# The S5 gate projection as seven block products, with its weight sums made in DRAM

## The chip, the cores and the metric

One core of one Trainium2 chip runs the whole layer. The metric is the device time of one execution in microseconds (us); the kernel before took 1628.49 us, the median of three runs (1626.33 to 1628.78).

## The reference

The kernel computes one decoder layer for 1024 tokens of width 1024, in float32: an S5 branch and an mLSTM branch side by side, merged by gates, then `w_out`, cross-attention to 256 memory tokens and a convolutional FFN. The part that the change touches, cut from the reference:

```python
h = _rmsnorm(x, mix_norm_g[l])
proj = h @ w_in[l]
u_s5, q_in, k_in, v_in, o_in, i_pre, f_pre, gate_pre = jnp.split(proj, split_points, axis=-1)
y_s5 = _s5(u_s5, ...)      # ends in y * sigmoid(y @ w_glu + b_glu)
y_m = _mlstm(q_in, k_in, v_in, o_in, i_pre, f_pre, ...)
gates = jax.nn.sigmoid((gate_pre + b_gate[l]).astype(jnp.float32)).astype(x.dtype)
g_s5, g_m = jnp.split(gates, 2, axis=-1)
merged = g_s5 * (y_s5 @ w_br_s5[l]) + g_m * (y_m @ w_br_m[l])
x = x + merged @ w_out[l]
```

`gate_pre` has 2048 columns: 1024 for the S5 branch and 1024 for the mLSTM branch.

## The kernel before

Activations lie transposed: a tile has 128 features in its partitions and the 1024 tokens along its free dimension. A float32 product is made of three fp32r products, high by high, high by low and low by high. `split` makes the two parts of an operand: ACT casts it to the high part, DVE subtracts that from it for the low part. The input h is kept as eight such pairs, `hx`, of x times its norm gain; the factor of the norm, a row `rb` of one number per token, is multiplied onto the product later.

`ntile` makes one output tile of 128 columns: `load_w` fetches 512 KB of weights by a DMA on SP's queue into a buffer `WR` and splits it into `WH` and `WL` (two buffers of each), and PE runs 8 blocks x 3 products x 2 halves of 512 tokens = 48 matmuls into `M`, a PSUM tile of 1024 columns of which there are two. With `nk=4` (`w_br`, `w_glu`, whose inputs are 512 wide) there are 24 matmuls and 256 KB. PSUM tiles `A` of 512 columns, four of them, serve the small products. S, R, Z, Y and VV are pools of SBUF tiles.

`gate_tile(i, n)` is one tile of `gate_pre` (i is 0 for S5, 1 for mLSTM): `ntile`, times `rb`, plus bias, sigmoid. `merge_tile(i, n)` takes such a gate and multiplies it by the tile of `y @ w_br`; for i = 0 it adds the mLSTM part and splits the sum for `w_out`.

The table `ORDER` lists the steps of the first part of the kernel: p, r the S5 scan in four parts (`s5_params`, `s5_run`), v, g, j, m the mLSTM (`v_half`, `gate_rows`, `proj_head`, `mlstm_head`), s and y splits of the branch outputs (`ym_split`; `y_load` fetches the S5 output from `Yd` in DRAM and applies Gelu), and a0 to a7 the mLSTM merges with their gates. Behind the table follow S5 gate tile 0, the four glu tiles, S5 gate tile 1 and the eight S5 merges, each with its gate tile ahead of it from the third on. From this order and a cost model a scheduler sets the fixed sequence of instructions on each engine; an engine runs its own list strictly in order, and so does each engine's list of DMA issues.

In the FFN, products of 2x2 blocks are already made as seven products for eight (`Uq` and `Dd` hold sums of weight quarters). `quad_sums` makes such sums in DRAM without an engine's arithmetic: four DMA copies of a quarter (512 KB each) on POOL's queue, then four DMAs that accumulate another quarter or an earlier sum onto them, the last two after one another. The copies are held back until `last_mm`, the last weight matmul written before them, is done. Before the change two sets of Uq follow a5 and a7, and the four of Dd the second, fourth, sixth and eighth S5 merge.

A line number of the new file is up to 10 higher than the old one ahead of the gate code and more behind it (`ntile`'s matmuls are L214 before and L224 after, `quad_sums` L850 and L853 before and L965 after).

Of the kernel before, what the change touches and what calls it, by code (L numbers as in the profile page):

```python
# [88 lines left out]
def hybrid_layer(ctx: ExitStack, tc: tile.TileContext, a):  # L91
# [124 lines left out]
    def ntile(src, xs, nk=KD, width=T):  # L216

        wh, wl = load_w(src, (nk, P))
        ps = psM()
# [575 lines left out]
        return ymt  # L795

    def gate_tile(i, n):
        ps = ntile(a["w_in"][13 + 8 * i + n], hx)
# [1 line left out]
        V.tensor_tensor(out=gt, in0=ps, in1=rb, op=ALU.mult)  # L800
        A.activation(out=gt, in_=gt, func=AF.Sigmoid, bias=col("b_gate", 8 * i + n))
# [4 lines left out]

    def merge_tile(i, n, ys, gt=None):
        gt = gt or gate_tile(i, n)
        pb = ntile(a["w_br"][i, n], ys, nk=4)
        if i == 1:  # L810
            merged.append([Y(), Y()])
            for j in range(2):
                hs = slice(512 * j, 512 * j + 512)
                V.tensor_tensor(out=merged[n][j], in0=gt[:, hs], in1=pb[:, hs], op=ALU.mult)
            return
        hi, lo = S(F32R) if n < 4 else Z(F32R), Halves([Y(F32R), Y(F32R)])
        for j in range(2):
# [2 lines left out]
            V.tensor_tensor(out=gt[:, hs], in0=gt[:, hs], in1=pb[:, hs], op=ALU.mult)  # L820
# [26 lines left out]
    def quad_sums(dst, src, jj, starts, sums, after, w=slice(0, T)):

        for i, q in enumerate(starts):
            d = nc.gpsimd.dma_start(out=dst[jj, :, i, w], in_=src[jj, :, q, w])  # L850
            tc.add_manual_dep(d.ins, after.ins.name, DependencyInfo(DependencyClass.Sync, DependencyReason.DATA), reason="pace")
        for i, q in enumerate(sums):
            nc.gpsimd.dma_start(out=dst[jj, :, i, w], in_=src[jj, :, q, w] if i < 2 else dst[jj, :, q, w], accum_op=ALU.add)  # L853
# [7 lines left out]
    def up_sums(g):  # L861
        quad_sums(Uq, a["w_uq"], g, (1, 0, 0, 2), (3, 1, 0, 2), last_mm[0])

    for step in ORDER:
        i = int(step[1])
        if step[0] == "p":
            prm[i] = s5_params(i)
        elif step[0] == "r":
            s5_run(i, *prm[i])
        elif step[0] == "v":  # L870
            v_half(i)
        elif step[0] == "g":
            gate_rows()
        elif step[0] == "j":
            hp[i] = proj_head(i)
        elif step[0] == "m":
            ymf[i] = mlstm_head(i, *hp[i])
        elif step[0] == "s":
            ym_split(i)
        elif step[0] == "y":  # L880
            y_load(i)
        else:
            merge_tile(1, i, [ym[h] for h in range(NH)])
            if step in UP_SUMS_AT:
                up_sums(UP_SUMS_AT.index(step))


    ysp = [ysp[j] for j in range(4)]
    early = [gate_tile(0, 0)]
    y2 = []  # L890
    for j in range(4):
        ps = ntile(a["w_glu"][j], ysp, nk=4)
        hi, lo = (S(F32R), S(F32R)) if j < 2 else (VV(F32R)[:, :T], VV(F32R)[:, :T])
        for i in range(2):
            hs = slice(512 * i, 512 * i + 512)
            A.activation(out=ps[:, hs], in_=ps[:, hs], func=AF.Sigmoid, bias=col("b_glu", j))
            y_ = ysp[j][2][:, hs]
            V.tensor_tensor(out=y_, in0=y_, in1=ps[:, hs], op=ALU.mult)
            split(hi[:, hs], lo[:, hs], y_)
        y2.append((hi, lo))  # L900
    early.append(gate_tile(0, 1))
# [766 lines left out]
```

## Time and profile before

| what | value |
|---|---|
| median of 3 runs | 1628.49 us (1626.33 to 1628.78) |
| the profiled execution | 1622.69 us, span 1620.9 us, mean granted clock 0.996 |
| PE busy | 1597.7 us, 99% of the span |
| DVE, ACT, POOL busy | 1056.6, 700.7, 144.1 us |
| mLSTM with the projections in it | about 155.8 to 330 us of the span |
| mLSTM merges and the last S5 part | about 330 to 445.1 us |
| S5 gates, glu, S5 merges | 445.1 to 597.7 us |
| w_out and cross-attention begin | 597.7 us |

The page is of one execution. The row of an instruction group reads: line, engine, operation, output tile <- input tiles, shape, count, then busy us and mean ns of one, then the idle time of that engine just before them with what ended it. A row of the timeline gives the start in us, the duration in us, the instruction and, in brackets, the idle time ahead of it. PE is TensorE, PEld its weight loads, DVE VectorE, ACT ScalarE, POOL GpSimd, SP SyncE.

### The profile page before, as it was taken

The page shows a single profiled execution, that of the slowest core. Times are in us where ns is not written, and L with a number is a line of the kernel's source. Part 1 is how long each engine was busy: PE and PEld are TensorE (multiplying, and loading weights), DVE is VectorE, ACT ScalarE, POOL GpSimd, SP SyncE. Part 2 cuts the span into 40 slices and gives each one's busy share as a digit, 9 for nine tenths or more (in the row PEclk, how much of TensorE's full clock was granted, in tenths as well). Part 3 has the DMA queues.
Part 4 walks back from the last instruction along what each step waited for, and adds up shares of the span by engine and source line. Part 5 has one row for each costly group of instructions (what it writes and reads, how often), then busy time and mean ns, then how long its engine had stood idle before and what let it go on. Part 6 is the DMA issues. An engine that isn't in the chain of part 4 may idle for free.

```text
span 1620.9 us, 20862 instructions
## 1 busy us (share of the span) xinstructions
PE 1597.7 (99%) x8031; PEld 1347.7 (83%) x8031; DVE 1056.6 (65%) x1698; ACT 700.7 (43%) x1153; POOL 144.1 (9%) x216
## 2 busy tenths in 40 slices
PE   9999999999999999999999999999999999999997
PEld 7898888888888888888888888888887888888887
DVE  7878767675344434344466468788889878867535
ACT  6446545633432223343354346444434445543423
POOL 0000000000111112100000000000111011221014
PEclk9999999999999999999999999999999999999998
DMA  5231211313665688953205244532677375886312
GB/s 198 95 97 57 79 53 59 86 46 104 175 156 149 161 252 240 292 132 107 97 29 206 104 156 163 198 108 78 190 183 196 109 181 172 309 284 207 119 39 105
DMA packets 87653, 233.83 MB, mean 144 GB/s; under 512 B 9601, under 2 KB 23617, under 8 KB 87553
## 3 DMA queue, kind: packets, MB, share of 16 engines
q1 hardware_dynamic: 58528, 138.73, 25.7%
q0 software_dynamic: 21488, 75.25, 18.7%
q10 hardware_dynamic: 7536, 18.52, 3.1%
q8 instruction: 63, 1.03, 0.3%
q14 instruction: 38, 0.30, 0.1%
HBM read 201.53 MB, written 85.46 MB: 177 GB/s over the span
## 4 chain that ended last, share of the span: by engine, by line
PE 93%; DVE 2%; issue 1%; DMA 1%; ACT 1%; SPq 0%; POOL 0%; POOLq 0%; DVEq 0%; ACTq 0%
PE M L214 41%; PE A L1208 14%; PE M L1208 10%; PE M L1352 6%; PE A L1352 5%; PE A L214 4%; PE M L299 1%; PE A L1074 1%; PE A L1020 1%; PE A L994 1%; PE M L614 1%; PE M L616 1%; PE M L615 1%; PE A L299 1%; DMA S<-in_w_up_dram 1%
## 5 line engine op out<-in xcount | busy, mean ns | idle before, releaser
L214 PE MATMUL M<-S,WH 128*128 128x512 f32 (+1 forms) x1704 | 459.6, 382 | 1.9 <-DVE dc L787 1.4
L214 PEld LDWEIGHTS M<-S,WH 128*128 128x128 f32 x1704 | 312.9, 188 | 63.0 <-issue 2.1
L214 PE MATMUL M<-S,WL 128*128 128x512 f32 (+1 forms) x884 | 277.5, 381 | 0.0
L186 ACT CAST WH<-WR 128x1024 fp32r<-128x1024 f32 (+2 forms) x107 | 99.4, 930 | 326.6 <-PE M L214 246.9
L214 PEld LDWEIGHTS M<-S,WL 128*128 128x128 f32 x884 | 165.8, 188 | 31.5 <-DVE WL L187 0.5
L187 DVE TENSOR_TENSOR WL<-WR,WH 128x1024 fp32r<-128x1024 f32 (+2 forms) x107 | 114.7, 1072 | 74.9 <-ACT WH L186 73.6
L1208 PE MATMUL M<-S,Y 128*128 128x512 f32 x468 | 112.2, 389 | 0.8 <-DVE Z L1221 0.8
L1208 PEld LDWEIGHTS M<-S,Y 128*128 128x128 f32 x468 | 87.8, 188 | 19.3 <-DVE Z L1221 1.1
L1231 DVE SCALAR_TENSOR_TENSOR S<-Z,cols,S 128x1023 f32<-128x1023 f32 (+1 forms) x72 | 90.8, 1278 | 7.2 <-ACT S L1229 7.2
L1208 PE MATMUL M<-S,W 128*128 128x512 f32 x324 | 78.3, 389 | 0.0
L186 ACT CAST W<-Y 128x512 fp32r<-128x512 f32 x51 | 31.4, 620 | 97.4 <-PE A L1208 67.4
L800 DVE TENSOR_TENSOR R<-M,R 128x1024 f32<-128x1024 f32 x16 | 19.6, 1222 | 82.6 <-PE M L214 82.6
L1208 PEld LDWEIGHTS M<-S,W 128*128 128x128 f32 x324 | 60.8, 188 | 12.6
L1208 PE MATMUL A<-S,W 128*128 128x512 f32 x288 | 70.6, 389 | 0.0
L1208 PEld LDWEIGHTS A<-S,W 128*128 128x128 f32 x288 | 54.1, 188 | 11.2
L1208 PE MATMUL A<-S,Y 128*128 128x512 f32 x240 | 60.1, 389 | 0.0
L1352 PE MATMUL M<-S,W 128*128 128x512 f32 x240 | 57.8, 389 | 0.0
L1208 PE MATMUL A<-R,W 128*128 128x512 f32 x228 | 56.5, 391 | 0.6 <-ACT Z L1215 0.5
L187 DVE TENSOR_TENSOR S<-S,S 128x512 fp32r<-128x512 f32 x79 | 51.8, 683 | 5.9 <-ACT S L186 5.8
L186 ACT CAST S<-S 128x512 fp32r<-128x512 f32 x79 | 46.4, 618 | 17.4 <-PE M L1352 6.1
L214 PE MATMUL A<-S,WH 128*128 128x512 f32 (+1 forms) x184 | 53.2, 372 | 0.5 <-ACT WH L186 0.5
L1208 PE MATMUL A<-VV,W 128*128 128x512 f32 x216 | 53.4, 389 | 0.0
(478 smaller groups left out, 3042.1 us busy)
## 6 DMA issues: line engine op xcount, KB each, us to landing
WR<-in_w_in_dram SPq DMA_DIRECT2D x29, 512.0 KB, 3.3
Uq<-in_w_uq_dram POOLq DMA_DIRECT2D x24, 512.0 KB, 9.0
Dd<-in_w_dq_dram POOLq DMA_DIRECT2D x24, 512.0 KB, 7.5
Td<-Gq POOLq DMA_DIRECT2D x24, 512.0 KB, 8.4
Gq<-S SPq DMA_DIRECT2D x18, 512.0 KB, 3.8
WR<-in_w_o_dram SPq DMA_DIRECT2D x16, 512.0 KB, 3.4
Y<-Uq SPq DMA_DIRECT2D x32, 256.0 KB, 3.9
S<-Td POOLq DMA_DIRECT2D x16, 512.0 KB, 5.4
```

What stands on the lines that cost most here:

```text
L186: A.copy(out=hi, in_=src)
L187: (lo_eng or V).tensor_tensor(out=lo, in0=src, in1=hi.bitcast(F32), op=ALU.subtract)
L214: last_mm[0] = PE.matmul(ps[:, s:e], lhsT, rhs[:, s:e], start=first and is_first, stop=last and is_last)
L299: PE.matmul(pus[j][h.start // 512], w_[:, 0, j * P : (j + 1) * P], x_[:, h], start=k == 0 and f, stop=k == KD - 1 and l)
L614: PE.matmul(ps, xh, wh, start=k == 0, stop=False)
L615: PE.matmul(ps, xh, wl, start=False, stop=False)
L616: PE.matmul(ps, xl, wh, start=False, stop=k == KD - 1)
L800: V.tensor_tensor(out=gt, in0=ps, in1=rb, op=ALU.mult)
L994: PE.matmul(pv[2 * m + j], lhsT, rhs[:, 0, 512 * j : 512 * j + 512], start=k == 0 and f, stop=k == KD - 1 and l)
L1208: up_mm[0] = PE.matmul(ps, lhsT[:, c], rhs, start=f, stop=l, skip_group_check=True)
L1231: V.scalar_tensor_tensor(out=acc[:, d_:], in0=raw[:, : T - d_], scalar=col("fcw", 3 * ct + 2 - d_), in1=acc[:, d_:], op0=ALU.mult, op1=ALU ...
L1352: paced[0] = PE.matmul(dps[p][n], lhsT[:, c], rhs, start=f, stop=l, skip_group_check=True)
```

## The change

The S5 half of `gate_pre` is computed by the scheme of seven products for 2x2 blocks (features even and odd tile, tokens first and second half, output columns even and odd tile), for two groups of four output tiles: step `e` followed by p and g is product p of group g. Products 1, 2 and 3 use `hx` as it is, 4 to 7 sums of x quarters. Each has 24 matmuls (2 column quarters x 4 blocks x 3), with two PSUM tiles A as the output; products 1 and 2 share them. The results are combined by DVE and ACT in SBUF (`gate_done` ends a half tile with `rb` and sigmoid), and the gates wait in S tiles, `gts`, for their merge.

`x_sums` (X0 to X3) loads x again, scales it on ACT with the gain, odd tiles negated, adds on DVE and writes the four kinds of sums to DRAM (`Xt`); `x_split` (T4 to T7) loads one kind back and splits it. The weights of products 1, 2 and 4 come from `w_gq`, laid out on the host from the same weights, the others from `Gw`, filled by `quad_sums`. MIX_SUMS says behind which step which phase of which sums is issued: G is Gw, U is Uq, the next digit the set, the last one the phase (0 the four copies, 1 to 3 the accumulations); D is a whole set of Dd. The glu tiles stand between the last e steps, and a merge is 24 matmuls with no gate tile ahead of it.

```diff
-UP_SUMS_AT = ("a5", "a7")
 ORDER = (
     "p0 r0 v0 p1 v1 g0 p2 r1 j0 m0 j1 m1 j2 m2 p3 s0 j3 m3 s1 s3 s2 y0 a0 a1 r2 a2 a3 r3 a4 y1 "
-    "y2 y3 a5 a6 a7 "
+    "X0 X1 a5 X2 X3 a6 a7 e10 e11 e20 T6 e21 T7 e30 T4 e31 T5 e60 e61 e70 y2 e71 y3 u0 e40 u1 e41 u2 e50 u3 e51 "
 ).split()
+MIX_SUMS = {
+    "m0": "G00 U00",
+    "j1": "G01 U01",
+    "m1": "G02 U02",
+    "j2": "G03 U03",
+    "m2": "G10 U10",
+    "j3": "G11 U11",
+    "m3": "G12 U12",
+    "s3": "G13 U13",
+    "e31": "D0",
+    "e71": "D1",
+    "u1": "D2",
+    "e50": "D3",
+}
...
+    def x_sums(i):
+        xe, xo = Z(), Z()
+        for t, k, g_ in ((xe, 2 * i, col("mix_g", 2 * i)), (xo, 2 * i + 1, ngain[:, 2 * i + 1 : 2 * i + 2])):
+            nc.sync.dma_start(out=t, in_=a["xT"][k])
+            A.activation(out=t, in_=t, func=AF.Copy, scale=g_)
+        e0, e1, o0, o1 = xe[:, :512], xe[:, 512:], xo[:, :512], xo[:, 512:]
+        for out, x, y, p in ((e0, e0, e1, 5), (e1, e1, o1, 7), (o1, o1, e0, 6), (o0, o0, o1, 4)):
+            V.tensor_tensor(out=out, in0=x, in1=y, op=ALU.add)
+            nc.sync.dma_start(out=Xt[p - 4, i // 2, :, i % 2], in_=out)
...
+    def gate_done(g, q, b, h, ps, t, sign):
...
+        if t is None:
+            V.tensor_tensor(out=c, in0=ps[q], in1=rbh, op=ALU.mult)
+        else:
+            V.tensor_tensor(out=c, in0=t[:, H[q]], in1=ps[q], op=ALU.add)
+            V.tensor_tensor(out=c, in0=c, in1=rbh, op=ALU.mult)
+        A.activation(out=c, in_=c, func=AF.Sigmoid, scale=sign, bias=col("b_gate", n))
...
+    def gate_job(p, g):
...
+        gate_weights(k + 1)
+        wh, wl = gws.pop((p, g))
+        if p != 2:
+            gps[g] = [psA(), psA()]
+        ps = gps[g]
+        for q in range(2):
+            for i in range(4):
+                c = slice(512 * q + P * i, 512 * q + P * i + P)
+                xh, xl = gx[p][i]
+                for w, x, f, l in ((wh, xh, i == 0 and p != 2, False), (wh, xl, False, False), (wl, xh, False, i == 3)):
+                    last_mm[0] = PE.matmul(ps[q], w[:, 0, c], x, start=f, stop=l, skip_group_check=True)
+        if p in (1, 3):
+            t = (gu if p == 1 else gr)[g] = S()
+            for q in range(2):
+                A.copy(out=t[:, H[q]], in_=ps[q])
...
+        elif p in (6, 7):
+            for q in range(2):
+                V.tensor_tensor(out=gu[g][:, H[q]], in0=gu[g][:, H[q]], in1=ps[q], op=ALU.subtract if p == 6 else ALU.add)
+            if p == 6:
+                V.tensor_tensor(out=gr[g], in0=gu[g], in1=gr[g], op=ALU.subtract)
...
     for n in range(KD):
-        merge_tile(0, n, y2, early[n] if n < 2 else None)
-        if n % 2:
-            down_sums(n // 2)
+        merge_tile(0, n, y2)
```

Three places in the order show what it moves. A name ends in the number of the buffer; rows read output <- input.

POOL during the mLSTM, before: the four `dc` are the powers that end a head (m0 to m3), the MEMSET clears the table kk of step p3.

```order
L495 MEMSET Y_1471 128x256
L786 TENSOR_TENSOR dc_1880<-dc_1880,mhalf 128x8
L786 TENSOR_TENSOR dc_2202<-dc_2202,mhalf 128x8
L786 TENSOR_TENSOR dc_2524<-dc_2524,mhalf 128x8
L495 MEMSET Y_2618 128x256
L786 TENSOR_TENSOR dc_2919<-dc_2919,mhalf 128x8
L850 DMA Uq<-in_w_uq_dram 128x1024 x4
```

After, from the second head's power on:

```order
L796 TENSOR_TENSOR dc_2218<-dc_2218,mhalf 128x8
L965 DMA Gw<-Gw 128x1024
L965 DMA Uq<-Uq 128x1024
L965 DMA Gw<-in_w_gq_dram 128x1024 x4
L965 DMA Uq<-in_w_uq_dram 128x1024 x4
L796 TENSOR_TENSOR dc_2544<-dc_2544,mhalf 128x8
L965 DMA Gw<-in_w_gq_dram 128x1024 x2
L965 DMA Uq<-in_w_uq_dram 128x1024 x2
L965 DMA Gw<-Gw 128x1024
L505 MEMSET Y_2646 128x256
L965 DMA Uq<-Uq 128x1024
L965 DMA Gw<-Gw 128x1024
```

The MEMSET and the powers now stand behind accumulations that wait for the ones before them.

ACT in the middle of the S5 gates, before: weight casts (WH), sigmoids of the gate tiles (L801) and splits of merged halves (S).

```order
L186 CAST WH_4387<-WR_4385 128x1024
L186 CAST S_4324<-Y_3093 128x512
L186 CAST S_4324<-Y_3094 128x512
L186 CAST WH_4445<-WR_4443 128x512
L186 CAST S_4366<-Y_3186 128x512
L186 CAST S_4366<-Y_3187 128x512
L186 CAST WH_4487<-WR_4485 128x1024
L801 ACTIVATE R_4440<-R_4440,cols 128x1024
```

After, from the copy out of product 3 of group 0: L889 copies a product from PSUM, L939 is the Gelu of y2 (Z_4453) and y3 (Z_4502), WH_4351 and WH_4386 are the weights of e61 and e70.

```order
L889 COPY S_4326<-A_4300 128x512
L196 CAST S_4338<-Z_4337 128x1024
L939 ACT_TABLE_LOAD
L939 ACTIVATE Z_4453<-Z_4453 128x1024
L196 CAST WH_4351<-WR_4349 128x1024
L889 COPY S_4326<-A_4301 128x512
L196 CAST S_4344<-Z_4343 128x1024
L939 ACTIVATE Z_4502<-Z_4502 128x1024
L196 CAST WH_4386<-WR_4384 128x1024
```

The two Gelu, which wait for loads from `Yd`, stand ahead of the casts of weights.

SP's queue at the S5 gates, before: weight loads alone, 512 KB and 256 KB in turn.

```order
L195 DMA WR_4385<-in_w_in_dram 128x1024
L195 DMA WR_4443<-in_w_br_dram 128x512
L195 DMA WR_4485<-in_w_in_dram 128x1024
L195 DMA WR_4543<-in_w_br_dram 128x512
L195 DMA WR_4593<-in_w_in_dram 128x1024
```

After, from the weights of e30 on: loads of Xt and Yd between them, all of 512 KB.

```order
L205 DMA WR_4151<-in_w_gq_dram 128x1024
L205 DMA WR_4199<-Gw 128x1024
L205 DMA WR_4247<-Gw 128x1024
L205 DMA WR_4294<-Gw 128x1024
L842 DMA Z_4282<-Xt 128x1024
L842 DMA Z_4288<-Xt 128x1024
L205 DMA WR_4349<-Gw 128x1024
L842 DMA Z_4337<-Xt 128x1024
L842 DMA Z_4343<-Xt 128x1024
L938 DMA Z_4453<-Yd 128x1024
L205 DMA WR_4384<-Gw 128x1024
L938 DMA Z_4502<-Yd 128x1024
```

The weights of e70 now stand in the queue behind the first load from `Yd`, which waits for a Z buffer.

More of the change, by code (lines that the diff above doesn't have):

```diff
@@ L797, in gate_tile @@
     def gate_tile(i, n):
-        ps = ntile(a["w_in"][13 + 8 * i + n], hx)
+        ps = ntile(a["w_in"][13 + n], hx)
         gt = R()
@@ L802, in gate_tile @@
         return gt
-    merged, mgs = [], []
-    def merge_tile(i, n, ys, gt=None):
-        gt = gt or gate_tile(i, n)
+    ngain = cp.tile([P, KD], F32, name="ngain")
+    G.tensor_scalar(out=ngain, in0=col("mix_g", 0, KD), scalar1=-1.0, scalar2=None, op0=ALU.mult)
+    Gw = dr.tile([NG, P, 4, T], F32, name="Gw")
+    Xt = dr.tile([4, 2, P, 2, 512], F32, name="Xt")
+    GW = {1: 0, 2: 2, 4: 3}
+    GS = {5: 0, 7: 1, 6: 2, 3: 3}
+    gx = {p: [None] * 4 for p in range(1, 8)}
+    for i in range(4):
+        for p, k, h in ((1, 2 * i, 0), (2, 2 * i + 1, 0), (3, 2 * i + 1, 1)):
+            gx[p][i] = tuple(t[:, 512 * h : 512 * h + 512] for t in hx[k])
@@ new lines, in hybrid_layer @@
+    gps, gu, gr, gws = {}, {}, {}, {}
+    def x_sums(i):
[7 more added lines that the diff above has]
+            nc.sync.dma_start(out=Xt[p - 4, i // 2, :, i % 2], in_=out)
@@ new lines, in x_split @@
+    def x_split(p):
+        for k in range(2):
+            raw, hi, lo = Z(), S(F32R), S(F32R)
+            nc.sync.dma_start(out=raw, in_=Xt[p - 4, k])
+            split(hi, lo, raw)
+            for i in range(2):
+                hs = slice(512 * i, 512 * i + 512)
+                gx[p][2 * k + i] = hi[:, hs], lo[:, hs]
+    H = H0, H1 = slice(0, 512), slice(512, T)
+    gts = {}
+    def gate_done(g, q, b, h, ps, t, sign):
+        n = 4 * g + 2 * q + b
+        if h == 0:
+            gts[n] = S()
+        c, rbh = gts[n][:, H[h]], rb[:, H[h]]
+        if t is None:
[4 more added lines that the diff above has]
+        A.activation(out=c, in_=c, func=AF.Sigmoid, scale=sign, bias=col("b_gate", n))
@@ new lines, in hybrid_layer, with gate_weights @@
+    gjobs = [(int(s_[1]), int(s_[2])) for s_ in ORDER if s_[0] == "e"]
+    def gate_weights(k):
+        if k < len(gjobs):
+            p, g = gjobs[k]
+            src = a["w_gq"][g, :, GW[p]] if p in GW else Gw[g, :, GS[p]]
+            gws[p, g] = load_w(src.unsqueeze(1), (1, T))
+    def gate_job(p, g):
+        k = gjobs.index((p, g))
+        if k == 0:
+            gate_weights(0)
+        gate_weights(k + 1)
[4 more added lines that the diff above has]
+        for q in range(2):
+            for i in range(4):
+                c = slice(512 * q + P * i, 512 * q + P * i + P)
[6 more added lines that the diff above has]
+                A.copy(out=t[:, H[q]], in_=ps[q])
+        elif p == 2:
+            for q in range(2):
+                gate_done(g, q, 0, 0, ps, None, 1.0)
+        elif p in (6, 7):
+            for q in range(2):
+                V.tensor_tensor(out=gu[g][:, H[q]], in0=gu[g][:, H[q]], in1=ps[q], op=ALU.subtract if p == 6 else ALU.add)
+            if p == 6:
+                V.tensor_tensor(out=gr[g], in0=gu[g], in1=gr[g], op=ALU.subtract)
+        else:
+            for b, h, t, sign in ((1, 0, gu[g], -1.0),) if p == 4 else ((1, 1, gu[g], 1.0), (0, 1, gr[g], -1.0)):
+                for q in range(2):
+                    gate_done(g, q, b, h, ps, t, sign)
@@ L809, in merge_tile @@
+    merged, mgs = [], []
+    def merge_tile(i, n, ys):
+        if i == 1:
+            gt = gate_tile(i, n)
+        else:
+            gt = gts[n]
         pb = ntile(a["w_br"][i, n], ys, nk=4)
@@ L841, in y_load, with glu_tile, quad_sums @@
         ysp[j] = (hi, lo, y)
+    y2 = []
+    def glu_tile(j):
+        ps = ntile(a["w_glu"][j], [ysp[k] for k in range(4)], nk=4)
+        hi, lo = (S(F32R), S(F32R)) if j < 2 else (VV(F32R)[:, :T], VV(F32R)[:, :T])
+        for i in range(2):
+            hs = slice(512 * i, 512 * i + 512)
+            A.activation(out=ps[:, hs], in_=ps[:, hs], func=AF.Sigmoid, bias=col("b_glu", j))
+            y_ = ysp[j][2][:, hs]
+            V.tensor_tensor(out=y_, in0=y_, in1=ps[:, hs], op=ALU.mult)
+            split(hi[:, hs], lo[:, hs], y_)
+        y2.append((hi, lo))
     Dd = dr.tile([NPP, P, 4, T], F32, name="Dd")
     Uq = dr.tile([NE // 2, P, 4, T], F32, name="Uq")
[L847 to L853, printed above, removed]
+    def quad_sums(dst, src, jj, starts, sums, after, w=slice(0, T), phases=(0, 1, 2, 3)):
+        for ph in phases:
+            for i, q in list(enumerate(starts if ph == 0 else sums))[{0: slice(0, 4), 1: slice(0, 2), 2: slice(2, 3), 3: slice(3, 4)}[ph]]:
+                d = nc.gpsimd.dma_start(out=dst[jj, :, i, w], in_=src[jj, :, q, w] if ph < 2 else dst[jj, :, q, w],
+                                        **({"accum_op": ALU.add} if ph else {}))
+                if ph == phases[0]:
+                    tc.add_manual_dep(d.ins, after.ins.name, DependencyInfo(DependencyClass.Sync, DependencyReason.DATA), reason="pace")
     def down_sums(jj):
@@ L881, in hybrid_layer @@
             y_load(i)
+        elif step[0] == "X":
+            x_sums(i)
+        elif step[0] == "T":
+            x_split(i)
+        elif step[0] == "u":
+            glu_tile(i)
+        elif step[0] == "e":
+            gate_job(i, int(step[2]))
         else:
             merge_tile(1, i, [ym[h] for h in range(NH)])
[L884 to L901, printed above, removed]
+        for job in MIX_SUMS.get(step, "").split():
+            kind, g, phases = job[0], int(job[1]), tuple(map(int, job[2:])) or (0, 1, 2, 3)
+            if kind == "D":
+                down_sums(g)
+            else:
+                quad_sums(*((Uq, a["w_uq"]) if kind == "U" else (Gw, a["w_gq"])), g, (1, 0, 0, 2), (3, 1, 0, 2), last_mm[0], phases=phases)
     for n in range(KD):
-        merge_tile(0, n, y2, early[n] if n < 2 else None)
-        if n % 2:
-            down_sums(n // 2)
+        merge_tile(0, n, y2)
     X1d = dr.tile([KD, P, T], F32, name="X1d")
@@ L1080, in hybrid_layer @@
     Cd = dr.tile([4, P, T], F32, name="Cd")
-    H = H0, H1 = slice(0, 512), slice(512, T)
     r3 = cp.tile([P, 8], F32, name="r3")
@@ L1596, in _layout @@
     o["memT"] = c(np.asarray(inp["mem"])[0].T.reshape(2, 4, P, 256).transpose(0, 2, 1, 3))
-    sel = np.concatenate([w_in[:, 384:1536], w_in[:, 2048:2560], w_in[:, 2568:4616]], axis=1)
+    sel = np.concatenate([w_in[:, 384:1536], w_in[:, 2048:2560], w_in[:, 3592:4616]], axis=1)
+    wg = w_in[:, 2568:3592].reshape(4, 2, P, 2, 2, 2, P).transpose(3, 2, 1, 5, 4, 0, 6)
+    o["w_gq"] = c(wg.reshape(2, P, 4, T))
     o["w_in"] = ntiles(sel)
```

1 line of the change is left out of this document (added).

## The prediction

> **What bounds the kernel.** I read first the busy times and the shares of the chain that ended last, then the table of the stretches that the change touches (columns: length, busy time of PE, weight loads, DVE, ACT and POOL with their counts, granted clock, DMA share, GB/s).
>
> ```profile
> span 1620.9 us, 20862 instructions
> PE 1597.7 (99%) x8031; PEld 1347.7 (83%) x8031; DVE 1056.6 (65%) x1698; ACT 700.7 (43%) x1153; POOL 144.1 (9%) x216
> PE 93%; DVE 2%; issue 1%; DMA 1%; ACT 1%; SPq 0%; POOL 0%; POOLq 0%; DVEq 0%; ACTq 0%
> ...
> 155.80:330.00 174.20, 172.79 (x1006) 148.74 (x1005) 124.46 (x219) 95.85 (x185) 6.87 (x5) 1.00 0.23 69
> 330.00:445.10 115.10, 114.00 (x563) 94.92 (x562) 63.83 (x101) 41.97 (x50) 5.66 (x8) 1.00 0.39 112
> 445.10:597.70 152.60, 152.60 (x674) 126.33 (x674) 64.61 (x89) 43.25 (x59) 21.50 (x32) 1.00 0.66 173
> 597.70:700.00 102.30, 102.26 (x451) 84.38 (x450) 48.66 (x75) 35.01 (x58) 20.76 (x31) 1.00 0.93 262
> ```
>
> PE is busy 99% of the span and makes 93% of the chain. The third stretch holds what is rewritten (eight S5 gate tiles, four glu tiles, eight S5 merges): PE is never idle there, so a matmul taken out is worth its whole length. The first stretch is the mLSTM, where PE idles 1.41 us and DMA is used at 0.23; the new weight sums go there. The chain of waits gives the price of a matmul in a dense run, the first row below; the second, from the waits between 280 and 450 us, is the longest that PE has there.
>
> ```profile
> 429.38 265.27 PE M L214 x1169
> PE M L214 <- DVE dc L787: 1.4, 1, 1.4
> ```
>
> 265.27 / 1169 = 0.2269 us per matmul; 24 are 5.44 us, 48 are 10.89 us.
>
> **What is removed.** 8 gate tiles of 48 are 384 matmuls; 7 products for 2 groups of 24 are 336. 48 fewer at 0.2269 us: −10.9 us, all on the path. No transpose or other PE work is added.
>
> **What DVE and ACT get.** These are rows of the third stretch and of the whole page (busy, mean ns of one | idle before).
>
> ```profile
> L820 DVE TENSOR_TENSOR R<-R,M 128x512 f32<-128x512 f32 x15 | 9.7, 684 | 23.0 <-PE M L214 23.0
> L801 ACT ACTIVATE R<-R,cols 128x1024 f32<-128x1024 f32 x8 | 9.2, 1155 | 5.8 <-DVE R L800 5.8
> L800 DVE TENSOR_TENSOR R<-M,R 128x1024 f32<-128x1024 f32 x8 | 9.8, 1224 | 52.9 <-PE M L214 52.9
> L186 ACT CAST WH<-WR 128x1024 fp32r<-128x1024 f32 (+2 forms) x107 | 99.4, 930 | 326.6 <-PE M L214 246.9
> L187 DVE TENSOR_TENSOR WL<-WR,WH 128x1024 fp32r<-128x1024 f32 (+2 forms) x107 | 114.7, 1072 | 74.9 <-ACT WH L186 73.6
> ```
>
> In the gate stage DVE gains 36 evictions and sums of 512 columns at 0.684 and 2 of 1024 at 1.224 (27.1 us), 8 subtractions of the operand splits at 1.224 (9.8) and 6 more weight subtractions at 1.072 (6.4), and loses eight L800 (9.8): 64.6 + 33.5 = 98 of the remaining 141.7 us. ACT: 6 weight casts at 0.930, 8 operand casts and 16 half sigmoids and 8 copies, at no more than 1.155 each, less 9.2: below 43.3 + 33.4 = 77. Neither becomes the bound on average: 0, hidden under PE. The sums over x (16 additions, 10.9 us of DVE, 8 scalings, 9.2 of ACT) stand beside the last mLSTM merges, in the end of the second stretch, which leaves 51 us of DVE and 73 of ACT free; their 8 MB of transfers take the place of 8 MB of Uq sums that were issued at steps a5 and a7: 0.
>
> **What the DMA queue of POOL gets.** The sums Gw and half of Uq move into the first stretch. What such sums do to POOL and to other transfers shows where they ran before (start, duration, wait in brackets; then median us from issue to landing: two Uq sets, the Z and w_br loads beside them, w_in and w_br loads and Dd accumulations between 495 and 600 us, w_out and w_q loads between 600 and 690, and at last over the whole page).
>
> ```profile
> 412.32 2.36 POOL L850 DMA_DIRECT2D Uq<-in_w_uq_dram  x4 [90.99 <-PE M L214]
> 417.26 0.88 POOL L853 DMA_DIRECT2D Uq<-in_w_uq_dram  x1 [2.59 <-DMA Uq<-in_w_uq_dram]
> 427.20 0.81 POOL L853 DMA_DIRECT2D Uq<-Uq  x1 [6.81 <-DMA Uq<-in_w_uq_dram]
> 499.87 2.08 POOL L850 DMA_DIRECT2D Dd<-in_w_dq_dram  x4 [31.86 <-PE M L214]
> 520.94 0.81 POOL L853 DMA_DIRECT2D Dd<-Dd  x1 [7.11 <-issue]
> ...
> Uq<-in_w_uq_dram POOLq DMA_DIRECT2D x10, 512.0 KB, 7.1
> Z<-Yd SPq DMA_DIRECT2D x1, 512.0 KB, 11.5
> ...
> WR<-in_w_in_dram SPq DMA_DIRECT2D x5, 512.0 KB, 3.3
> WR<-in_w_br_dram SPq DMA_DIRECT2D x5, 256.0 KB, 8.1
> Dd<-Dd POOLq DMA_DIRECT2D x6, 512.0 KB, 7.1
> ...
> WR<-in_w_out_dram SPq DMA_DIRECT2D x5, 512.0 KB, 8.5
> WR<-in_w_q_dram SPq DMA_DIRECT2D x2, 512.0 KB, 9.1
> ...
> WR<-in_w_br_dram SPq DMA_DIRECT2D x16, 256.0 KB, 2.8
> ```
>
> One copy or accumulation lands after about 7.1 us; POOL waits 2.6 to 6.8 us for the one before a dependent accumulation, and a load that meets the copies takes 8 to 11.5 us instead of 2.8 to 3.3. POOL's own mLSTM work is small but stands behind these in its queue:
>
> ```profile
> 207.72 1.64 POOL L786 TENSOR_TENSOR dc<-dc,mhalf 128x8 f32<-128x8 f32 x1 [87.18 <-DVE dc L785]
> 285.07 0.32 POOL L495 MEMSET Y<- 128x256 f32 x1 [12.67 <-DVE Y L362]
> ...
> 243.57 1.22 DVE L706 TENSOR_TENSOR S<-M,R 128x1024 f32<-128x1024 f32 x1 [1.44 <-PE M L214]
> 246.34 0.42 SPq L719 DMA_DIRECT2D Y<-Rd  x1
> 247.81 0.38 SPq L720 DMA_DIRECT2D Y<-Rd  x1
> 287.11 1.20 DVE L706 TENSOR_TENSOR S<-M,R 128x1024 f32<-128x1024 f32 x1
> 292.61 0.33 SPq L719 DMA_DIRECT2D Y<-Rd  x1
> ...
> Y<-Rd SPq DMA_DIRECT2D x12, 256.0 KB, 5.4
> DVE Y L721 <- DMA Y<-Rd: 1.4, 1, 1.4
> ...
> 214.85 1.04 PE L793 MATMUL A<-ident,Y 128*128 128x128 f32 x8
> 294.66 0.32 PE L504 MATMUL A<-S,Y 128*32 128x16 f32 x16
> ```
>
> (1) Step m2's four row loads go at 246.3 to 247.8, some 3 us after the last matmul of step j2 (its eviction, L706, starts at 243.57) releases two accumulations and eight copies, 20 us of traffic by the interval from 499.87 to 520.94 for four copies and what follows. They took 5.4 us and DVE already waited 1.4 us for one (the last but two of these rows); beside copies 8 to 11.5 us, 2.7 to 6 more. The heads' own matmuls stand between projection tiles, so some of it is covered. Ends 0 and 5; I take 1.5, since the loads start after the first copies are under way and PE has another tile's matmuls ahead.
> (2) The MEMSET of the table kk for the fourth S5 part stands behind an accumulation that is gated at the end of j3 (about 286.2 us, just ahead of its eviction at 287.11) and waits for its predecessor: 286.2 + 2.1 for issuing + 7.1 to 8, about 296 to 297, plus 1.0 us of ACT copies. PE needed it at 294.66, and in the new order 12 to 13 matmuls later (2.9 us), 297.6. Ends 0 and 3.3 (PE stalls for everything behind it); I take 1.0.
> (3) The first dc (207.72, pow) stands behind the second set's accumulations, so about 2.5 us later, but PE uses its result at 214.85: 0, ends 0 and 3.
> (4) Step m3's row loads from 292.61 on meet eight copies: 0.5, ends 0 and 3.
>
> **What the gate stage's loads get.** Weight buffers are double. The cast and subtraction of a tile start when the one but last is through its matmuls, and take 0.93 + 1.07 and about 0.3 of hand-over, 2.3 us, of 5.44 until it's needed (before, of 10.89). A load may take 2 x 5.44 − 2.3 = 8.6 us; with L above that, the period is (L + 2.3) / 2.
> (5) Around e61 and e70 two Gelu of y2 and y3, whose loads from Yd are issued as the sums D0 begin, stand on ACT ahead of the casts of these weights. With 11.5 us for a Yd load they come some 6 us late, with the 3.3 of the w_in loads not at all. Ends 0 and 6; I take 1.5, nearer the lower end, as the w_in loads of the same stage kept 3.3 us beside the sums.
> (6) Merges now follow each other with 24 matmuls and nothing between: DVE has per tile 0.68 of weight subtraction, 4 x 0.684 of merging and 2 x 0.69 of splits, 4.8 of 5.44 us, and w_br loads at 8.1 of 8.6 us. Ends 0 and 3; I take 0.5.
>
> By the Trainium skill ("DMA: Bandwidth & Descriptors", Queues, rings and completion order) each DMA engine takes the rows that have work in turn, packet by packet, so that an SP load beside POOL's copies should lose no more than half of its rate: the 3.3 us would become at most about 6.6, below 8.6, and the terms 5 and 6 were 0 (sum −7.9). The trace doesn't agree, 2.8 us became 8.1, and I keep them.
>
> **Sum:** −10.9 + 1.5 + 1.0 + 0 + 0.5 + 1.5 + 0.5 = −5.9 us, so a span of 1615.0 and 1616.8 us for the profiled execution (1622.69 before). That one lies 5.8 us below the median of the runs shown, 1628.49; with the same distance the median becomes 1622.6 us.
>
> **Rivals.** *All hidden:* each row load and the MEMSET falls into slack: −10.9, with the mLSTM's 1.41 us of idle at best −12.3: 1616.2 to 1618.9, 1617.6 as its centre. For it: the DMA share of 0.23 in that stretch; against: the loads at 8 to 11.5 us beside sums.
>
> *Eaten in the mLSTM:* terms 1 and 2 come at their upper ends, 5 and 3.3, the others as taken: −0.1, 1628.4. For it: PE order is fixed, so a late row load stops all behind it; against: before, PE waited for one single row 1.4 us. The Trainium skill ("TensorE: Matmul & The Clock Gate", What's actually happening) halves the clock after some 3.4 us of idle PE, for as long; by that a stall of 5 us would cost about 1.7 more. No stretch here shows a clock under 1.00, as none has such a stall.
>
> *Slower, by the pace of the weight loads:* from the end of e31 on, the sums D0 to D3 follow each other without a gap (one takes 520.94 − 499.87 + 7.1 = 28 us; four 113), beside some 20 tiles of 24 matmuls. At 11.5 us per load the period is 6.9, +1.46 us a tile: +29 − 10.9 = +18, 1646. It decides where the tiles lose 10.9 / 20 = 0.54 us each, at loads of 9.7 us. For it: 8.1, 8.5, 9.1 and 11.5 above, on nearly as dense sums; against: 3.3 for w_in, and that only a sum's copies, not its later accumulations, are four deep.
>
> **Numbers.** All hidden 0.22; the likeliest, 1618.9 to 1625.2, 0.40; eaten, within 0.2% (3.3 us, about what a measurement of this kernel can tell from no change; 1625.2 to 1631.7), 0.20; above that 0.18, most of it the loads' pace or several upper ends at once (all of them: +12.4). So faster 0.62, same 0.20, slower 0.18. The range from 1616.8 to 1631.5 leaves out 0.18 above and little below; the likeliest one's own is 1618.9 to 1625.2.
>
> **What would show it.** The third stretch's work should end within 141 to 145 us with some 48 matmuls less and PE idle under 4 us, with waits on weight splits or Gelu near e61 only. In the mLSTM, PE idle should grow from 1.4 to some 4 us, behind the row loads of m2 (DVE's addition L721, L731 in the new file) and before the matmuls on kk. Loads of weights beside D0 to D3 should land within 8.6 us. I am wrong if the mLSTM idles over 8 us, if PE waits for weight splits tile after tile, or if a later stage, in which the order is unchanged, moves by more than 2 us.

## The result and the profile after

The changed kernel takes 1640.82 us, the median of four runs (1636.57 to 1642.01), against 1627.41 us for the kernel before in the same comparison: a ratio of 1.0079 (95% interval 1.0056 to 1.0102), slower. The forecast was 1622.6 us, 1616.8 to 1631.5. The profiled execution took 1641.88 us with a span of 1640.1. The spans of the two profiled executions differ by 19.2 us, the medians by 13.4: the profiled one of the kernel before (1622.69 us) is faster than its median by 4.7, that of the changed kernel slower by 1.1. The stretches below add up to the 19.2.

The page of the changed kernel: span, busy times, shares of the chain that ended last.

```profile
span 1640.1 us, 20986 instructions
PE 1599.4 (98%) x7983; PEld 1345.9 (82%) x7983; DVE 1097.3 (67%) x1758; ACT 729.3 (44%) x1192; POOL 155.6 (9%) x233
PE 87%; DMA 6%; DVE 3%; issue 2%; ACT 2%; SPq 0%; POOL 0%; ACTq 0%; POOLq 0%; DVEq 0%
```

There are 48 matmul records fewer (7983, not 8031), and yet PE is busy for 1.7 us longer; DMA now makes 6% of the chain, not 1% (2.7 of it are loads of x in w_out, 2.3 the row loads below). I divided the two spans at the same events (the evictions that follow j2, j3, the gates of the second and the last mLSTM merge, the last S5 merge and the sixth of the eight w_out tiles, each the start of the same DVE instruction in either trace):

| stretch up to | before, us | after, us | difference |
|---|---|---|---|
| j2's eviction | 243.6 | 244.8 | +1.2 |
| j3's eviction (m2 lies in it) | 43.5 | 54.4 | +10.9 |
| gate of the second mLSTM merge (m3 lies in it) | 34.3 | 43.0 | +8.7 |
| gate of the last mLSTM merge | 118.3 | 118.1 | −0.2 |
| last S5 merge (the rewritten stage) | 158.4 | 155.2 | −3.2 |
| sixth w_out tile | 67.8 | 70.3 | +2.5 |
| end | 955.0 | 954.3 | −0.7 |

The stretches of the mLSTM and of the gate stage, of the changed kernel (columns as in the prediction's table):

```profile
244.80:299.20 54.40, 47.04 (x240) 39.94 (x239) 32.84 (x53) 22.78 (x45) 7.68 (x12) 0.94 0.51 141
299.20:342.20 43.00, 36.16 (x222) 30.71 (x220) 20.17 (x43) 20.34 (x46) 6.82 (x9) 0.92 0.85 179
460.30:615.50 155.20, 151.31 (x652) 122.55 (x651) 100.95 (x137) 70.85 (x97) 21.62 (x32) 0.99 0.82 227
...
260.00:270.00 10.00, 5.11 (x22) 4.02 (x20) 3.11 (x7) 3.85 (x10) 0.00 (x0) 0.83 0.97 301
270.00:280.00 10.00, 7.53 (x35) 6.46 (x36) 8.06 (x11) 4.54 (x9) 0.00 (x0) 0.83 0.25 90
```

The stretch from j2 to j3 before:

```profile
243.60:287.10 43.50, 43.50 (x239) 37.52 (x238) 33.52 (x52) 20.87 (x42) 1.95 (x2) 1.00 0.18 55
```

PE was never idle between j2 and j3; now it is idle for 7.4 us (54.40 − 47.04), and the matmuls that are left take 47.0 instead of 43.5 us, since the granted clock falls to 0.83 beside and behind the idle time. PE's busy time grows by 5.5 us in the two stretches of the mLSTM (47.04 + 36.16, before 43.50 + 34.23) and falls by 7.1 in the gate stage (151.31, before 158.40). The chain of waits says for what PE waits, once in m2 and once in m3, and the waits name the same places (4.3 us in m2, where 2.3 and 0.8 more follow at L775 and L782; 6.8 in m3):

```profile
249.34 21.28 DMA Y<-Rd
311.98 16.99 DMA Y<-Rd
...
PE A L768 <- DVE Y L769: 6.8, 1, 6.8
PE A L768 <- DVE Z L761: 4.3, 1, 4.3
```

L768 are the heads' products; DVE prepares their operands from the row loads (`Y<-Rd`, 256 KB each). m2's four go out from 247.56 to 249.34 us, when two accumulations and six of the eight copies have been issued on POOL's queue (the last two follow at 251.5 and 255.2). m3's first goes at 304.05, the other three from 310.97 on; ahead of them are not copies but the four accumulations of the next phase and a dependent one:

```profile
245.29 0.87 POOL L965 DMA_DIRECT2D Gw<-Gw  x1 [3.37 <-PE M L224]
246.42 2.66 POOL L965 DMA_DIRECT2D Gw<-in_w_gq_dram  x4
248.49 1.61 POOL L965 DMA_DIRECT2D Uq<-in_w_uq_dram  x2
...
299.03 1.75 POOL L965 DMA_DIRECT2D Gw<-in_w_gq_dram  x2 [13.62 <-PE M L224]
300.18 2.26 POOL L965 DMA_DIRECT2D Uq<-in_w_uq_dram  x2
```

How long transfers took from issue to landing between 240 and 275 us (medians), in the changed kernel and, last line, before:

```profile
Gw<-in_w_gq_dram POOLq DMA_DIRECT2D x4, 512.0 KB, 15.7
Uq<-in_w_uq_dram POOLq DMA_DIRECT2D x4, 512.0 KB, 22.5
Y<-Rd SPq DMA_DIRECT2D x4, 256.0 KB, 15.5
...
Y<-Rd SPq DMA_DIRECT2D x4, 256.0 KB, 4.8
```

The row loads land with the copies, not beside them. So far this is a reading of one trace; the experiments take the suspects away one by one.

### The profile page after: what moved, and what is told of

Read it like the earlier page. It is cut to its first block, busy times and chain, and to the rows that moved or that the text cites. A ratio compares the mean times of both kernels' runs of the same rounds, so it can differ in the third digit from the quotient of the medians.

```text
span 1640.1 us, 20986 instructions
## 1 busy us (share of the span) xinstructions
PE 1599.4 (98%) x7983; PEld 1345.9 (82%) x7983; DVE 1097.3 (67%) x1758; ACT 729.3 (44%) x1192; POOL 155.6 (9%) x233
## 4 chain that ended last, share of the span: by engine, by line
PE 87%; DMA 6%; DVE 3%; issue 2%; ACT 2%; SPq 0%; POOL 0%; ACTq 0%; POOLq 0%; DVEq 0%
PE M L224 31%; PE A L1318 15%; PE M L1318 11%; PE M L1462 6%; PE A L1462 4%; PE A L224 4%; PE A L885 3%; DMA S<-in_xT_dram 3%; DMA Y<-Rd 2%; PE M L309 1%; PE A L1185 1%; PE A L1131 1%; PE A L1105 1%; PE M L624 1%; PE M L626 1%
## 5 line engine op out<-in xcount | busy, mean ns | idle before, releaser
L224 PE MATMUL M<-S,WH 128*128 128x512 f32 (+1 forms) x1448 | 392.0, 382 | 4.1 <-DVE dc L794 1.4
L224 PEld LDWEIGHTS M<-S,WH 128*128 128x128 f32 x1448 | 265.2, 189 | 56.4 <-ACT WH L196 3.0
L224 PE MATMUL M<-S,WL 128*128 128x512 f32 (+1 forms) x756 | 238.5, 381 | 0.0
L196 ACT CAST WH<-WR 128x1024 fp32r<-128x1024 f32 (+2 forms) x113 | 105.8, 937 | 277.6 <-PE M L224 170.5
L197 DVE TENSOR_TENSOR WL<-WR,WH 128x1024 fp32r<-128x1024 f32 (+2 forms) x113 | 121.9, 1079 | 94.6 <-ACT WH L196 93.5
L224 PEld LDWEIGHTS M<-S,WL 128*128 128x128 f32 x756 | 142.1, 189 | 26.1
L885 PE MATMUL A<-S,WH 128*128 128x512 f32 x224 | 67.8, 393 | 0.2 <-ACT WH L196 0.2
```

The source lines that it names most:

```text
L196: A.copy(out=hi, in_=src)
L197: (lo_eng or V).tensor_tensor(out=lo, in0=src, in1=hi.bitcast(F32), op=ALU.subtract)
L224: last_mm[0] = PE.matmul(ps[:, s:e], lhsT, rhs[:, s:e], start=first and is_first, stop=last and is_last)
L885: last_mm[0] = PE.matmul(ps[q], w[:, 0, c], x, start=f, stop=l, skip_group_check=True)
```

## The experiments

Each run is compared with the kernel before on its own chip (there 1622.9 to 1623.7 us), so ratios are compared, and stretches within the profiles. My theory: the bytes of bursts that meet the row loads cost the 19.6 us in the mLSTM, and the weight loads beside D0 to D3 the 7.7 us that the gate stage falls short of 10.9. Rivals: POOL's queue order, and the gate stage's own order.

**An eighth of the bytes** of Gw's and Uq's sums in the mLSTM, in the same queue places; the sums stay incomplete and their readers take plain quarters of the weights.

```diff
-    quad_sums(..., last_mm[0], phases=phases)
+    quad_sums(..., last_mm[0], w=slice(0, 128), phases=phases)
```

> Every DMA of the weight sums Gw and Uq during the mLSTM stays in its place on POOL's queue, with its waits, but moves 128 of 1024 columns, an eighth of the bytes; the sums are incomplete, and the products read plain weight quarters from DRAM instead. Theory of the bytes (m2's and m3's row loads wait until the copies' traffic is through, and the idle PE then loses clock): row loads land in 5 to 7 us instead of 21 and 17, PE does not wait at L768, no stretch of the mLSTM under clock 1.00, and the time falls by 18 to 21 us from 1640.8 to 1620 to 1623. Rival, POOL's queue (the dc powers and the MEMSET stand behind accumulations that wait): the order and most of the waits are left, so at least half of the loss is left, 1631 or more.

Ratio 0.9990 (0.9972 to 1.0007). The same two stretches, and the row loads:

```profile
244.70:288.10 43.40, 43.40 (x239) 37.45 (x238) 33.23 (x53) 20.92 (x42) 7.57 (x12) 1.00 0.26 71
288.10:322.50 34.40, 34.34 (x223) 29.20 (x221) 20.10 (x43) 22.27 (x50) 7.01 (x9) 1.00 0.52 117
...
Y<-Rd SPq DMA_DIRECT2D x4, 256.0 KB, 6.6
```

All 19.6 us are gone and the clock is 1.00, with every DMA instruction still in its place: bytes, not queue order alone. The accumulations land sooner too (`Gw<-Gw` in 2.8 us, not 5.9), so this run leaves POOL's queue shorter as well; but no POOL instruction is in the chain of m2, and its first row load went out 2.8 us after j2's eviction, as before. The gate stage is still short: 154.5 us between the same two evictions, −3.9 to before.

**Uq's two sets back behind a5 and a7**, Gw alone in the mLSTM.

```diff
-    "m0": "G00 U00",  ...  "j2": "G03 U03",  "m2": "G10 U10",  ...
+    "m0": "G00",  ...  "j2": "G03",  "m2": "G10",  ...  "a5": "U0",  "a7": "U1",
```

> The two sets of Uq go back behind a5 and a7, as in the kernel before; Gw stays in the mLSTM. The burst at the end of j2 and j3 is half as large. Theory of the bytes: the row loads of m2 and m3 land in about half of 21 and 17 us (8 to 11), PE waits 0 to 3 us for each, and the time is 1640.8 - 19 + 0 to 6 + 0 to 3 for the Uq copies that now meet the loads of x: 1622 to 1630. Rival, POOL's queue: the same dependent accumulations are ahead of dc and MEMSET, so over half of the 19 us stays: 1632 or more.

Ratio 1.0062 (1.0043 to 1.0081), slower than I expected. In the mLSTM the theory holds for m2: with half the burst, the stretch up to j3 loses 5.3 us instead of 10.9, m3's nothing.

```profile
Gw<-in_w_gq_dram POOLq DMA_DIRECT2D x4, 512.0 KB, 11.1
Y<-Rd SPq DMA_DIRECT2D x4, 256.0 KB, 14.7
...
PE A L887 <- ACT WH L198: 6.3, 3, 3.9
```

But the row loads still took 14.7 us, and I had given too little for the other place: the Uq sums met the loads of x and the first 24-matmul products, PE waited 6.3 us there for weights, and the stretch from the gate of the second mLSTM merge to the last S5 merge is 6.3 us longer than in the changed kernel. The time is in the rival's range, but not for its reason: of the 19.6 us in the mLSTM only 5.3 are left, less than half.

**D0 to D3 behind S5 merges 1, 3, 5 and 7.**

```diff
-    "e31": "D0",  "e71": "D1",  "u1": "D2",  "e50": "D3",
...
     merge_tile(0, n, y2)
+    if n % 2:
+        down_sums(n // 2)
```

> The four sums Dd go back behind the S5 merges 1, 3, 5 and 7; all else as in the changed kernel. Theory of the loads' pace (the gate stage loses 7.7 of its 10.9 us since weight loads of 24-matmul tiles meet the copies of D0 to D3): that stage wins 4 to 7 us, some of it lost again where the copies now meet w_br and w_out loads: 1634 to 1638. Rival (the stage loses by its own order: Gelu of y2 and y3, Xt loads ahead of weights): no change, 1639 to 1642.

Ratio 1.0171 (1.0151 to 1.0191): the wrong direction, though the gate stage did win 3.4 us: 151.8 instead of 155.2, PE idle 2.7 us and the clock at 1.00.

```profile
456.60:608.40 151.80, 149.06 (x653) 121.60 (x652) 100.59 (x137) 69.89 (x96) 10.95 (x18) 1.00 0.51 159
574.44 2.14 POOL L961 DMA_DIRECT2D Dd<-in_w_dq_dram  x4 [232.37 <-PE M L220]
733.36 0.81 POOL L961 DMA_DIRECT2D Uq<-Uq  x1 [8.21 <-issue]
...
PE A L1112 <- POOL rm L248: 5.9, 1, 5.9
```

I had overlooked that "behind the merges" is another time now: the merges follow each other at the stage's end, so D0 begins at 574.4 us, not at 499.9 as before. The sums behind it in the queue end with an accumulation of Uq at 733.4. The stretches up to the sixth w_out tile and from there to the first tile of the attention's output are 7.5 and 10.2 us longer than before. PE is idle in the second alone (13 us, before 1.9), and its longest wait there, 5.9 us, is for `rm`, a power on POOL that stands right behind that accumulation.

**Both: D behind the merges, Uq behind the last tiles of cross-attention** (Gw alone in the mLSTM).

```diff
+        if step in ("a0", "q7"):
+            up_sums(int(step == "q7"))
```

> Dd behind the merges as in d_late, and the two sets of Uq behind the last k and q tile of cross-attention, where DMA is used at 0.06; Gw alone stays in the mLSTM. If the losses add up as the two theories say (row loads behind copies 19 us, weight loads behind D 4 to 7 us): 1640.8 - 16 - 5 = 1620, 1616 to 1624, faster than before. Rival (four copies hold the row loads as long as eight, or the late Uq copies meet the loads of attention): 1626 to 1634.

Ratio 1.0098 (1.0079 to 1.0117), no gain. ("d_late" is the run before this one.) It shows POOL's queue, which the mLSTM's loss did not need, at work elsewhere, with twice the wait of the run before. The longest wait of PE, and POOL at that time:

```profile
PE A L1112 <- POOL rm L248: 12.1, 1, 12.1
...
718.38 0.81 POOL L961 DMA_DIRECT2D Uq<-Uq  x1 [5.16 <-DMA Uq<-in_w_uq_dram]
726.53 0.81 POOL L961 DMA_DIRECT2D Uq<-Uq  x1 [7.34 <-issue]
727.09 1.00 POOL L248 TENSOR_TENSOR rm<-ms,mhalf 128x2 f32<-128x2 f32 x1
```

`rm`, a power of two columns, the norm factor of the memory tokens, for which PE waits, stands behind accumulations that wait for one another. The order is that of before; only the sums ahead of it are later.

**The same sums, released between the row loads.** All bytes stay in the mLSTM. The copies of a set go when the last row of m0 or m1 has been used, the accumulations at the end of the first tile of a j step or when a later head's rows have been used.

```diff
+    pace[f"m{h}"] = V.tensor_tensor(out=q_, in0=qt[...], in1=q_, op=ALU.mult)
...
-    quad_sums(..., last_mm[0], phases=phases)
+    quad_sums(..., pace.get(step, last_mm[0]), phases=phases)
```

> All sums of Gw and Uq stay in the mLSTM with all their bytes, but the phases are released at other points: the copies when a head's row loads have landed (the DVE instruction that uses the last row of m0 and m1), the accumulations at the end of the first tile of a j step or after the rows of m2 and m3. So no burst meets a row load. Theory (the loss is a collision of bursts and row loads): from j2's last eviction to j3's 43.5 to 45 us (54.4 in the changed kernel, 43.5 before), first to second mLSTM merge about 21 us, ratio to before 0.998 to 1.002. Rival (that much traffic within the mLSTM costs in any place, by weight loads or the S5 loads): 1.005 or more.

Ratio 0.9994 (0.9978 to 1.0009): against the changed kernel's 1.0079 some 14 us won by moving the time of release alone. From j2's to j3's eviction it took 46.9 us, more than I expected, though 12 matmuls more lie in that stretch and 12 fewer in the next. What is left of the loss in the mLSTM, 2.9 us up to the gate of the second merge against before, goes with slower row loads (10.1 us between 240 and 275) and with m2's power on POOL, which now did stand behind an accumulation; this run doesn't part the two:

```profile
273.93 0.81 POOL L968 DMA_DIRECT2D Uq<-Uq  x1 [6.59 <-DMA Uq<-in_w_uq_dram]
274.48 1.96 POOL L799 TENSOR_TENSOR dc<-dc,mhalf 128x8 f32<-128x8 f32 x1
```

**Row loads written earlier, into R tiles**, with the sums as in the changed kernel.

```diff
-            d_, q_ = Y(), Y()
+            w_ = R()
+            d_, q_ = w_[:, :512], w_[:, 512:]
```

> The sums stay as in the changed kernel; the four row loads of a head are written at the start of its j step and go into two R tiles instead of four Y tiles, so that in SP's queue the rows of m2 stand one or two weight loads earlier. Theory: rows that are loaded ahead of the burst cost nothing, those still behind it some: the stretch from j2 to j3 loses at most 4 of the 10.9 us, ratio 1.000 to 1.005. Rival (R tiles, four in all and also used for the raw products, become the wait): 1.006 or more.

Ratio 1.0116 (1.0084 to 1.0148). The rival's number came; that the four R tiles, which also hold the raw products, are the cause I have only argued. From j0's to j1's eviction the kernel takes 53.9 us instead of 39.8. In the two stretches of the bursts PE is idle for 3.5 and 3.0 us instead of 7.4 and 6.8, as the theory would have it, but with everything ahead of them moved I don't count that as shown.

**An eighth of the bytes in D0 to D3 too.**

```diff
-    quad_sums(Dd, ..., both_of(jj))
+    quad_sums(Dd, ..., slice(0, 128) if jj < 4 else both_of(jj))
```

> As in the kernel with an eighth of the bytes in Gw's and Uq's sums, and the same for the four sums D0 to D3, whose readers take plain quarters instead. It leaves all instructions and nearly no traffic of the sums. Theory of the loads' pace: the gate stage wins the 4 to 5 us that moving D away won, w_out 1 to 2: ratio 0.994 to 0.997, near the 0.993 that 10.9 us would be. Rival (the stage loses its 7 us by its own order of casts, Gelu, table loads and evictions): 0.998 to 1.000.

Ratio 0.9970 (0.9955 to 0.9984). The gate stage falls to 151.1 us, 3.4 us less than with D's bytes.

```profile
441.90:593.00 151.10, 148.39 (x650) 121.22 (x649) 100.69 (x138) 70.56 (x97) 21.86 (x32) 1.00 0.47 136
```

So of the 7.7 us about half are D's traffic; 3.6 us (151.1 − 158.4 + 10.9) are left with nearly no traffic at all. PE is idle 2.7 us in this row, for a weight cast behind the table load of u0's sigmoid (1.3 us) and for evictions and weight splits on DVE; that points to the stage's own order. The other 0.9 is PE's own busy time (148.39, where 158.4 less 10.9 is 147.5), and I can't place it.

**That table load earlier**, on the kernel with the sums between the rows.

```diff
         A.activation(out=y, in_=y, func=AF.Gelu_apprx_tanh)
+        if j == 3:
+            A.activation(out=small([P, 1], "sigw"), in_=y[:, :1], func=AF.Sigmoid)
```

> The kernel with the sums released between the row loads (ratio 0.9994), and one ACT instruction more: a sigmoid of one column of y3 right behind its Gelu, so that the table load for the sigmoid comes there and not between the weight cast of e41 and that of the second glu tile. Theory (this table load of 1.28 us makes PE wait 1.3 us, and the clock is then half for some 3 us): about 2.5 us less, ratio 0.997 to 0.9985, no stretch under clock 1.00 around u0. Rival (the cast waits for the weight buffer in any case): 0.999 to 1.000.

Ratio 1.0005 (0.9991 to 1.0020): nothing won. The wait of 1.3 us disappeared from PE's list, and the chain then went through the next weight load:

```profile
514.00 1.06 ACT WH L195
515.08 1.24 DVE WL L196
516.34 9.50 DMA WR<-Gw
```

Here, with double buffers, the weight tile that came early only met the next load, which took 9.5 us beside D's copies.

**D0 one product later, so that y3's load from Yd goes ahead of it.**

```diff
-    "e31": "D0",
+    "e60": "D0",
```

> As the kernel with the early table load, and D0 is released one product later, behind e60, so that the load of y3 from Yd goes before its copies. Theory: the wait for the weights of e70 (1.2 us in the changed kernel) goes, and the later sums move by 5 us: 0 to 2 us less than with the table load alone. Rival: D0 to D3 and D4 end later and the loss comes back in w_out: 0 to 2 us more.

Ratio 0.9991 (0.9978 to 1.0003). It overlaps with the former (1.0005); the stage is 2.7 us shorter in the profile (152.3 against 155.0), as the theory has it, but the runs don't separate the two. The same profile shows how far single ones go: with the same code in the mLSTM, j2 to j3 took 49.4 us here and 46.6 in the former.

**Uq's second set after m2's rows, later accumulations after m3.**

```diff
-    "m1": "G02 U02 G10 U10",  "j2": "G03 U03",  "m2": "G11 U11",  "j3": "G12 U12",  "m3": "G13 U13",
+    "m1": "G02 U02 G10",  "j2": "G03 U03",  "m2": "G11 U10",  "m3": "G12 U11",  "s3": "G13 U12",  "a0": "U13",
```

> As the kernel with the sums released between the row loads, but the copies of the second Uq set start after the rows of m2 instead of m1, and its accumulations and those of Gw's second set after m3's rows, step s3 and step a0, so that no accumulation that waits stands ahead of m2's dc power. In the former that power ran at 274.5 us right behind an accumulation (273.9), and m2's row loads took 10 us. Theory (bytes at the rows and POOL's queue before dc cost the 2.9 us that the mLSTM still loses): 1.5 to 3 us less, ratio 0.9975 to 0.9985. Rival (what is left there is scheduling of DVE and ACT): 0.999 to 1.000.

Ratio 0.9983 (0.9970 to 0.9995). The row loads between 240 and 275 us are back at 5.6 us, and j2 to j3 at 43.4 us. The ratio is the expected one, but its interval overlaps that of the kernel that it starts from (0.9978 to 1.0009). (Its profiled execution, 1628.86 us, is 9 us above the median of its runs, 1619.85; I read no more from it than the mLSTM.)

**All three together.**

> All three changes together: sums released as in the kernel before this one in the list, early table load, D0 behind e60. If they add up: 0.9994 - 0.0015 - 0.0015 - 0.0006 = 0.9958, 0.994 to 0.9975. If the gains share a cause or the later sums collide in w_out: 0.998 or more.

Ratio 0.9979 (0.9968 to 0.9990): 3.4 us faster than the kernel before by its ratio, 1620.01 us against 1623.22. The gains don't add up to the 0.9958 that I expected, and against the former run alone (0.9983) the other two changes show nothing. The mLSTM loses nothing with all the bytes of the sums in it, and the gate stage is 4.6 us shorter than before (158.4 to 153.8):

```profile
244.40:287.90 43.50, 43.50 (x239) 37.52 (x239) 33.46 (x53) 20.94 (x42) 5.81 (x8) 1.00 0.52 140
287.90:322.30 34.40, 34.36 (x222) 29.07 (x220) 20.61 (x45) 24.02 (x51) 5.92 (x6) 1.00 0.78 169
440.40:594.20 153.80, 149.84 (x653) 121.70 (x653) 100.72 (x137) 71.02 (x98) 21.56 (x32) 1.00 0.81 229
```

## Why the prediction was wrong

- **48 matmuls less, −10.9 us:** right as a price of PE's work; the gate stage gave back 7.7 of it. In the prediction's own bounds, from the last mLSTM merge to the last S5 merge, it took 149.1 us instead of 141 to 145.
- **Term 1, m2's row loads (1.5, ends 0 and 5): this step failed.** It measured 10.9 us. I priced a load "beside copies" with 8 to 11.5 us from rows where four copies had been issued, and here two accumulations and six copies were ahead of the last row. The row loads took 4.8 us without copies, 6.6 with an eighth of the bytes, 14.7 with four copies and 15.5 with eight (medians of four); the longest, on which the chain hangs, took 5.1, 7.2, 14.9 and 21.3. The cover that I named, another tile's matmuls, was not there either: PE's fixed order reached the head's products before the operands came. And 3.5 of the 10.9 us are not waiting at all but the lower clock behind it. That halving I had weighed in a sentence on the Trainium skill only ("TensorE: Matmul & The Clock Gate", What's actually happening), with 1.7 us. The trace agrees that the clock falls behind such a stall, granted clock 0.83 over the 20 us with the stall, but that is 6.8 us at half the clock (20 x 0.17 / 0.5), twice what I had taken from the rule.
- **Term 4, m3's row loads (0.5, ends 0 and 3):** the same step, 8.7 us. The term also misread the change: what m3's rows met were the accumulations of the next phase, not eight copies.
- **Terms 2 and 3, MEMSET and dc behind POOL's accumulations:** the first at 1.0 was 0, no wait for kk in the changed kernel's list (its sum, 286.2 + 2.1 + 7.1 to 8, makes 295.4 to 296.3, not 296 to 297). The first dc started 4.5 us later (212.23, before 207.72), 3.3 of them its own, and cost nothing. That the queue can cost showed in other orders (5.9 and 12.1 us for `rm`).
- **Terms 5 and 6, weight loads (2.0 together):** the waits that they name came near their size, 1.2 us for the weights of e70 behind the Gelu of y3 and 0.8 at the merges. But the stage lost 7.7 us. The sum lacked the table load (1.3 us), the halved clock behind it (below) and some 2 us of longer busy time that stay open. By the runs 3.4 of the 7.7 are D's bytes. The averages of DVE (101 of 155 us) and ACT (71) were as forecast and said nothing about it.
- **w_out, which I gave nothing:** +2.5 us, but PE loses none of it there. It is never idle in that stretch in either trace, and 12 matmuls more lie in it; the eviction that ends it waits for a load of x while PE goes on. What the change loses behind the gate stage is 1.8 us (2.5 − 0.7), and where stays open.

```profile
598.10:665.90 67.80, 67.80 (x300) 56.14 (x300) 27.88 (x41) 19.47 (x28) 14.98 (x23) 1.00 0.91 258
615.50:685.80 70.30, 70.30 (x312) 58.22 (x311) 27.88 (x40) 19.52 (x29) 10.02 (x15) 1.00 0.68 195
...
673.76 11.96 DMA S<-in_xT_dram
```

- **The 1.2 us ahead of j2's eviction** are not the change's either. They arise in the first 12 us: the matmuls take 0.63 us each up to 9.7 us of the span and 0.39 from 10.0 on, where the kernel before is at 0.39 from 6.1 us on. (The clock has no record earlier than 4.3 us before and 10.0 after, so that its column shows 1.00 for this, too.) Before and after:

```profile
4.00:12.00 8.00, 6.96 (x32) 5.27 (x31) 4.45 (x7) 6.07 (x10) 0.74 (x3) 1.00 0.96 354
4.00:12.00 8.00, 7.24 (x24) 5.68 (x23) 4.64 (x7) 5.69 (x10) 0.72 (x3) 1.00 0.99 352
```

The other profiles fall into the same two groups (29 to 33 matmuls, or 22 to 25); without the two that lose time elsewhere ahead of it, j2's eviction lies at −0.5 to 0.0 us in the first and at +0.9 to +1.9 in the second.
- **The rival on the slower side** that I named (weight loads at 11.5 us, +18) was the wrong mechanism at nearly the right sum; that was luck. The one that came true, "eaten in the mLSTM", I had stopped at −0.1, since the upper end of its term was 5.
- The Trainium skill's rule of turns between queue rows ("DMA: Bandwidth & Descriptors", Queues, rings and completion order) would at most have doubled a load. Here 4.8 us became 15.5 in the median, so the measurement decides against that use of it, as the rows before already did.

## What to carry to other kernels

A transfer on which a chain waits must be priced by the bytes that stand ahead of it when it is issued, not by the time that a like transfer took beside a smaller burst; then look at when the burst is released, since moving that moment, with all the bytes kept, won back the whole loss of the mLSTM here. A rule such as "behind the second merge" is a place in an order and not a time: when the change moves that place, everything that was released there moves with it, and the queue's later users too. A saving of 0.7% of the busy time of a PE that is 99% busy was in no run here worth its full price of 10.9 us: the stage that got shorter won 7.3 at most, with nearly no traffic of the sums beside it. Its tiles are half as long and ask for weights twice as often. And where a stretch ends with an eviction that waits for something else, count the matmuls in it before calling a longer stretch a loss.
